# mLSTM decay matrix, state scaling and gating queued behind later VectorE work; five weight parts ahead and later row rounding at the FFN's edges

## The chip, the cores and the metric

The kernel runs on one core of a Trainium2 chip. The metric is the device time of one execution in microseconds (us). Engine names are those of the profile: PE is TensorE's matmul, PEld its weight load, DVE is VectorE, ACT is ScalarE, POOL is GpSimd, SP is SyncE, which here only issues DMAs. Each engine works through its own queue of instructions, whose order is fixed when the kernel is built.

## What is computed

One inference step of a two-layer decoder, for 1024 new prompt tokens and 8 decode tokens, in float32. Layer 0 mixes tokens with an mLSTM, layer 1 with multi-head latent attention (MLA); each is followed by a SwiGLU FFN. Cut to what the change touches:

```
def mlstm_chunk(C, n, m, q, k, v, i_pre, log_f):          # one chunk, one head
    b = cumsum(log_f)
    log_intra = where(causal, b[:, None] - b[None, :] + i_pre[None, :], -inf)
    m_t = maximum(b + m, max(log_intra, -1))
    s = (q @ k.T) * exp(log_intra - m_t[:, None])          # decay matrix times scores
    num = exp(b + m - m_t) * (q @ C) + s @ v
    den = exp(b + m - m_t) * (q @ n) + sum(s, -1)
    h = num / maximum(abs(den), exp(-m_t))
    C = w_C * C + k.T @ (w_s * v)                          # state update
...
h = rmsnorm_per_head(h) * g_head
y = (sigmoid(o) * h) @ w_out                               # gating, output projection
...
def swiglu(x): g, u = split(x @ w_gate_up); return (silu(g) * u) @ w_down
```

The decode tokens scale and update a stored state per request in the same way.

## The kernel before, in words

**Precision.** Each float32 operand of a matmul is split into a rounded high part (ScalarE, line 117) and a rest (VectorE, line 118; with a gain factor lines 120 and 121); a product is three matmuls, high by high, low by high, high by low (`mm3`, lines 134 to 136). So every weight tile costs a load on SyncE's queue, a ScalarE and a VectorE operation before PE can use it. PE accumulates in PSUM, from which VectorE or ScalarE must copy a result before its bank is used again.

**Order of the work.** The program is written in one thread of Python. The framework builds each engine's queue from it: the instructions of one engine are put in an order by the program's order and by when an estimate says that their inputs are ready, so an instruction whose inputs are thought to be there early can be queued ahead of earlier work. On the chip this order is then fixed. `tc.issue_after(ins)` adds an ordering edge: what the block issues on the engine of `ins` is queued behind `ins`. It does not wait for `ins` to finish, and it binds no other engine.

**mLSTM.** After the projections of q, k and v (`proj_v(0..7)`, eviction at line 447), 16 chunk steps run: 8 chunks of 128 tokens by 2 groups of 4 heads (loop in `mlstm`, step `mlstm_chunk`). A step
- takes `Gb`, gate values broadcast to all partitions by a DMA on ScalarE's queue (`decay`, line 608; four buffers), and makes the decay matrix in place: four VectorE operations (line 625), then an exponential on ScalarE (line 626);
- multiplies the scores, fresh in PSUM, into it (line 633), turns k and v (kt, line 639; vn, line 645), and makes numerator and denominator on PE (lines 660, 662);
- updates the state C (PE line 672, VectorE lines 676 or 678, four operations);
- normalises: denominator (687 to 692), an inverse square root of eleven short operations (198 to 203), line 694, and the scaled output `hn` (line 697);
- in the next step, turns `hn` back on PE (701) and copies it over v (702).

Between the steps PE works on other products: in steps 1 to 8 the output gate's projection `proj_o` (three PSUM results in two banks, evicted at line 464, tanh at 465, stored by DMA), in steps 9 to 14 tiles of the output projection for the first 512 tokens (`op_tile`, line 863). The decode tokens' state is worked on in between by a generator, `mlstm_sample`: load the state of a request, scale it (line 799), add the new outer product (800), store it (801), and take its product with q (781). The gating of half 1 of the tokens (`gated`, lines 480, 120, 121) runs in steps 12 to 14, three, three and two heads, each loaded (`loaded`, line 475) just before.

**FFN.** The gate and up products use a Strassen-like scheme: per block of 128 columns (`f`, 22 of them) seven products (`PRODUCTS`) of seven weight parts (`operands`, which makes sums of weight quarters at lines 1032, 1033, 1038, 1039 and splits them) with seven sums of the activations, the "forms" (`forms`, lines 943 and 946, split at 117 and 118). The seven products share two PSUM banks per half of the tokens, so the first product's result must be copied out (line 1078) before the third starts the same bank again, and the second's (line 1080) before the fourth. The first two blocks are done without forms (`gate_up_half`); in `out_proj` the parts of block 2 are made among the forms of half 1, and `gate_up` takes them from `self.early`. The last four blocks (`fs`, 18 to 21) go a simpler way: `keep` splits their activations (ScalarE and VectorE) for a plain last product.

Of the kernel before, what the change touches and what calls it, by code (L numbers as in the profile page):

```python
# [13 lines left out]
ALU = mybir.AluOpType  # L14
# [4 lines left out]
P = 128  # L19
# [9 lines left out]
NF = DFF // P  # L29
# [62 lines left out]
class Kern:  # L92
# [309 lines left out]
    def mlstm(self, xz, rs, early):  # L402
# [41 lines left out]
        turned = self.gates(p1, pg, gi, lf, bcol)  # L444
        def proj_v(j):
            def ev(c, cs, ps):
                nc.vector.tensor_tensor(v[:, j, cs], ps, rs[:, cs], op=ALU.mult)
            proj(1024 + j * P, ev)

        for j in range(8):  # L450
            proj_v(j)
            if j == 4:
                turned()
        pg.release()
        o_d = self.t(self.dp, [P, 8, T], "o_d")
        pi = self.pool("mi")
# [17 lines left out]
        def loaded(og, i, h, zs):  # L474
            nc.sync.dma_start(og, o_d[:, h, 512 * i + zs.start:512 * i + zs.stop])
            return og, i, h, zs

        def gated(og, i, h, zs):
            cs = slice(512 * i + zs.start, 512 * i + zs.stop)
            nc.vector.scalar_tensor_tensor(og, og, 1.0, v[:, h, cs], op0=ALU.add, op1=ALU.mult)  # L480
            self.split(z[i][0][:, h, zs], z[i][1][:, h, zs], og, self.gcol(self.G_HEAD + h))


        smp = self.mlstm_sample(ms, q, k, v)
        last = None
        first, rest = OPC[1]
        due = [self.decay(pi, 0, 0)]
        for i in range(16):
            if i < 15:
                due.append(self.decay(pi, (i + 1) // 2, (i + 1) % 2))  # L490
            g = self.mlstm_chunk(pi, i // 2, i % 2, q, k, v, *due.pop(0))
            next(g)
            if i == 8:
                next(smp, None)
            if 1 <= i <= 8:
                proj_o(i - 1)
            elif 9 <= i <= 14:
                self.op_tile(0, i - 9, ("mm",))
            if last:
                next(last, None)  # L500
            last = g
            for _ in range(0 if i > 8 else 2 if i == 3 else 1):
                next(smp, None)
            if i == 8:
                ms.release()
                self.rp.release()
                self.zp.release()
                z = self.half_z(512)
                og = self.t(self.xq, [P, KT, 512], "x")
                for h in range(8):  # L510
                    gated(*loaded(og[:, h], 0, h, slice(0, 512)))
                self.op_open(self.mlstm_w_out[0], z)
                self.X[0] = self.t(self.xq, [P, KT, 512], "x")
                self.SS[0] = self.t(self.xq, [P, 512], "ss")
                self.sq[0] = self.xq
                self.op_residual(0, nc.sync)

            if 12 <= i <= 14:
                for h in range(3 * i - 36, min(8, 3 * i - 33)):
                    gated(*loaded(ob()[:, :256], 1, h, first))  # L520

        tiles = [self.t(pi, [P, 4, L], "Gb", bufs=4).rearrange("p h t -> p (h t)")] + [ob() for _ in range(3)]
        tiles += [self.t(pi, [P, 4, 129], "vn", bufs=3).rearrange("p h t -> p (h t)") for _ in range(2)] + [ob() for _ in range(2)]
# [91 lines left out]
    def mlstm_chunk(self, pi, c, hg, q, k, v, Gb, wb):  # L615
# [5 lines left out]
        a_t, ws_t, em_t = (self.tok[:, c, r, h4] for r in range(3))  # L621

        E = Gb
        for h in range(4):
            V.scalar_tensor_tensor(E[:, h], Gb[:, h], a_t[:, h:h + 1], self.ct[:, C_MM:C_MM + P], op0=ALU.subtract, op1=ALU.max)
        nc.scalar.activation(E, E, AF.Exp, scale=-1.0)
        for hh in range(2):
            ps = self.mmt("sc")[:, :2 * L]
# [44 lines left out]
        for h in range(4):  # L673
            r = slice((h % 2) * 64, (h % 2) * 64 + 64)
            if c == 0:
                V.tensor_copy(C[r, h], ps[r, h // 2])
            else:
                V.scalar_tensor_tensor(C[r, h], C[r, h], wc[r, h // 2:h // 2 + 1], ps[r, h // 2], op0=ALU.mult, op1=ALU.add)
        if c == NCK - 1:
            for hh in range(2):  # L680
                r = slice(hh * 64, hh * 64 + 64)
# [22 lines left out]
    def mlstm_sample(self, pi, q, k, v):  # L704
# [91 lines left out]
        for b in range(NS):  # L796
            yield
            Ct, vb = nxt
            V.tensor_tensor(Ct, Ct, wsb[:, 0, b].unsqueeze(2).to_broadcast([P, 4, P]), op=ALU.mult)
            V.tensor_tensor(Ct, Ct, vb, op=ALU.add)  # L800
            nc.sync.dma_start(self.C_s[0, b].rearrange("(q r) d e -> (r d) q e", r=2), Ct)
            if prev:
                products(*prev)
            if b < NS - 1:
                nxt = fetch(b + 1)
            prev = (b, Ct)
# [66 lines left out]
    def out_proj(self, layer):  # L873
        nc = self.nc
        V = nc.vector
        self.fz = self.pool("fz")
        xp = self.pool("xp")
        for i in range(1, -layer, -1):
            self.X[i] = self.t(xp, [P, KT, 2 * PW[i]], f"x{i}")
        nt = self.pool("nt")  # L880
        for i in range(1 - layer, 2):
            self.SS[i] = self.t(nt, [P, 2 * PW[1]], f"ss{i}")
            self.sq[i] = nt
        self.F = {}
# [24 lines left out]
        self.fc = self.pool("fc", side="right")  # L909
        self.nf = self.pool("nf", side="right")  # L910
        gen = self.forms(1, self.X[1], self.SS[1], g0)
        self.u = {}
        self.nr = self.no = 0
        wg = self.ffn_w_gate_up[layer]
        self.gate_up_half(wg, 0, gen)
        self.gate_up_half(wg, 1)
        ops = self.operands(wg, 2)
        parts = []
        for step in range(5):
            next(gen, None)  # L920
            parts += [next(ops) for _ in range((0, 2, 1, 1, 0)[step])]
        self.early = ops, parts
        self.nf.release()
        nt.release()
        xp.release()
# [119 lines left out]
    def gate_up(self, wg, f, parts, down=iter(()), skip=0, steps=(1, 1)):  # L1045
# [9 lines left out]
            ops = self.operands(wg, f)  # L1055
            ahead = [next(ops) for _ in range(2 if f < 3 else 1)]
        for s, bank, first in PRODUCTS:
            ahead.append(next(ops, None))
            w = ahead.pop(0)
            for i in parts:  # L1060
                pw = PW[i]
# [13 lines left out]
                    X[i] = self.t(gu, [P, PW[1]], "gt", bufs=2)[:, :pw]  # L1075
                u, x = U[i], X[i]
                if s == 0:
                    nc.scalar.copy(u[:, 0], ps)
                elif s == 4:
                    V.tensor_tensor(u[:, 0], u[:, 0], ps, op=ALU.add)  # L1080
                    nc.scalar.activation(u[:, 0], u[:, 0], AF.Silu)
# [113 lines left out]
    def ffn(self, layer):  # L1195
# [27 lines left out]
            o = lambda x: x[:, 512 * i:512 * i + 2 * PW[i]].rearrange("p (c t) -> p c t", c=2)  # L1223
            self.split(o(self.act[f][0]), o(self.act[f][1]), self.u[f, i])

        for i in range(2):
            keep(fs[0], i)
        self.gate_up(wg, fs[2], (0, 1), (keep(fs[1], i) for i in range(2)))
        self.gate_up(wg, fs[3], (0, 1))
        for f in fs[2:]:  # L1230
            for i in range(2):
# [831 lines left out]
```

## Time and profile before

| | us |
|---|---|
| median of 3 runs | 2632.49 |
| lowest and highest | 2632.12, 2639.99 |
| profiled execution: its own time | 2652.47 |
| its span, first to last instruction | 2650.7 |
| PE busy | 2520.7 |
| VectorE busy | 1861.4 |
| ScalarE busy | 1326.0 |

How to read the profile. A row of the timeline gives start, duration, engine, line, operation, out<-in by the program's names, shape, count, and in square brackets how long the engine was idle before it and what ended that. A row of waits gives who waited for whom, the total, the number of times and the longest. A row of stretches gives length, and the busy time of each engine with its number of instructions, then the granted clock of TensorE as a share of full speed, and the DMA engines' share and rate. The chain of waits follows the work that ended last back to what released it. PE's ends are modelled, and some matmul records can be missing.

### The profile page before, as it was taken

How to read it: one execution, taken by the hardware profiler on the slowest of the kernel's cores; microseconds unless marked ns; L12 is line 12 of the kernel's file. 1: busy time of each engine (PE TensorE's matmuls, PEld its weight loads, DVE VectorE, ACT ScalarE, POOL GpSimd, SP SyncE). 2: the span in 40 equal slices, each digit the busy share in tenths (PEclk: the TensorE clock that was granted, in tenths of full speed). 3: DMA queues.
4: the chain of work that ended last, by engine and by line, in shares of the span. 5: the costliest groups of instructions: out<-in, count | busy, mean ns of one | idle time of the engine just before them, and what ended most of it. 6: DMA issues, size and time to landing. Idle time of an engine off the chain costs nothing.

```text
span 2650.7 us, 54288 instructions
## 1 busy us (share of the span) xinstructions
PE 2520.7 (95%) x21151; PEld 2377.0 (90%) x21151; DVE 1861.4 (70%) x4491; ACT 1326.0 (50%) x3281; POOL 570.8 (22%) x588
## 2 busy tenths in 40 slices
PE   8998989999999999999988888988999999999998
PEld 8998977999999999999976667767899999999998
DVE  4345668897777777566657766767597877777755
ACT  4122234456565666454344454645355665656543
POOL 1001102202111111122335444541210111111102
PEclk9999999999999999999989999999999999999999
DMA  5123444527666566554657666664634656665653
GB/s 192 40 68 89 135 136 128 164 65 139 133 124 129 113 118 134 113 161 149 203 209 255 208 225 234 223 240 134 199 94 107 133 117 128 128 133 113 124 127 115
DMA packets 343128, 382.88 MB, mean 144 GB/s; under 512 B 23465, under 2 KB 275502, under 8 KB 334550
## 3 DMA queue, kind: packets, MB, share of 16 engines
q0 software_dynamic: 58688, 180.35, 29.2%
q1 hardware_dynamic: 258982, 182.30, 22.8%
q10 hardware_dynamic: 25200, 16.75, 2.4%
q8 instruction: 166, 2.72, 0.4%
q14 instruction: 92, 0.75, 0.1%
HBM read 253.63 MB, written 125.70 MB: 143 GB/s over the span
## 4 chain that ended last, share of the span: by engine, by line
PE 73%; DVE 11%; DMA 7%; ACT 5%; issue 3%; POOL 1%; SPq 0%; another core or an unknown queue 0%; ACTq 0%; POOLq 0%; DVEq 0%
PE sc L134 13%; PE sc L136 13%; PE sc L135 13%; PE mm L134 6%; PE mm L136 5%; PE mm L135 5%; PE ss L1873 2%; PE ss L134 2%; PE ss L136 2%; PE ss L135 2%; DVE tt L1841 2%; DMA Gb<-G_d 2%; PE ss L1848 2%; DVE wl L118 1%; PE mm L1744 1%
## 5 line engine op out<-in xcount | busy, mean ns | idle before, releaser
L1178 POOL DMA_DIRECT2D x_d<-wl x72 | 86.8, 1205 | 1001.8 <-DVE wl L1177 347.1
L117 ACT ACTIVATE wh<-wr 128x512 fp32r<-128x512 f32 (+2 forms) x167 | 133.4, 800 | 179.9 <-PE mm L135 111.0
L1841 DVE STREAM_TRANSPOSE tt<-nat 128x1024 f32<-128x1024 f32 x128 | 153.9, 1223 | 16.7 <-PE ss L1848 13.0
L118 DVE TENSOR_TENSOR wl<-wr,wh 128x1024 fp32r<-128x1024 f32 (+2 forms) x80 | 93.0, 1164 | 27.1 <-ACT wh L117 26.4
L134 PE MATMUL mm<-zh,wh 128*128 128x344 f32 x320 | 104.4, 326 | 6.5 <-DVE ot L464 6.5
L118 DVE TENSOR_TENSOR b<-u,b 128x256 fp32r<-128x256 f32 (+1 forms) x252 | 103.2, 423 | 9.2 <-ACT b L117 7.8
L117 ACT ACTIVATE b<-u 128x256 fp32r<-128x256 f32 (+1 forms) x252 | 99.0, 415 | 15.8 <-PE ss L136 6.3
L1178 POOL DMA_DIRECT2D x_d<-st x72 | 104.6, 1453 | 5.0 <-DVE dC L118 3.8
L1848 PE MATMUL ss<-tt,qbd 128*32 128x128 f32 x2560 | 94.0, 280 | 11.8 <-issue 6.3
L118 DVE TENSOR_TENSOR wh<-S,wh 128x512 fp32r<-128x512 f32 x108 | 74.6, 691 | 42.9 <-ACT wh L117 42.8
L135 PE MATMUL mm<-zl,wh 128*128 128x344 f32 x320 | 103.5, 324 | 0.0
L136 PE MATMUL mm<-zh,wl 128*128 128x344 f32 x320 | 103.3, 323 | 0.0
L1848 PEld LDWEIGHTS ss<-tt,qbd 128*32 128x32 f32 x2560 | 72.2, 112 | 29.5 <-issue 12.9
L117 ACT ACTIVATE wh<-S 128x512 fp32r<-128x512 f32 x108 | 68.0, 630 | 59.6 <-PE sc L136 39.7
L1744 PE MATMUL mm<-wh,vt 128*128 128x256 f32 (+1 forms) x320 | 79.4, 309 | 10.0 <-ACT wh L117 5.6
L134 PE MATMUL sc<-zh,wh 128*128 128x344 f32 x256 | 83.5, 327 | 2.9 <-ACT wh L117 2.7
L136 PE MATMUL sc<-zh,wl 128*128 128x344 f32 x256 | 82.7, 323 | 0.7 <-DVE wl L118 0.7
L135 PE MATMUL sc<-zl,wh 128*128 128x344 f32 x256 | 82.7, 323 | 0.0
L1873 PE MATMUL ss<-nat,pz 128*32 128x256 f32 x1024 | 68.6, 401 | 11.2 <-ACT pz L1869 10.6
L1703 ACT ACTIVATE wr<-sc,mx,rqt 128x512 f32<-128x512 f32 (+2 forms) x96 | 64.2, 674 | 26.8 <-DVE mx L1698 13.1
L1744 PEld LDWEIGHTS mm<-wh,vt 128*128 128x128 f32 x320 | 58.0, 205 | 21.7 <-ACT wh L117 9.7
L1833 POOL DMA_INDIRECT nat<-in_cache_latent_dram,idx x64 | 60.8, 950 | 75.2 <-PE ss L1873 61.5
(1078 smaller groups left out, 10666.1 us busy)
## 6 DMA issues: line engine op xcount, KB each, us to landing
wr<-in_ffn_w_gate_up_dram SPq DMA_DIRECT2D x96, 512.0 KB
x_d<-st POOLq DMA_DIRECT2D x72, 520.0 KB
x_d<-wl POOLq DMA_DIRECT2D x72, 512.0 KB
dr<-in_ffn_w_down_dram SPq DMA_DIRECT2D x72, 256.0 KB
wr<-in_mlstm_w_in_dram SPq DMA_DIRECT2D x24, 512.0 KB
wr<-in_mlstm_w_out_dram SPq DMA_DIRECT2D x16, 512.0 KB
q<-qn_d SPq DMA_DIRECT2D x28, 256.0 KB
wr<-in_mla_w_o_dram SPq DMA_DIRECT2D x14, 512.0 KB
```

What stands on the lines that cost most here:

```text
L117: ins = nc.scalar.activation(hi, src, AF.Copy)
L118: self.low = e.tensor_tensor(lo, src, hi.bitcast(F32), op=ALU.subtract)
L134: mm(ps, wh, xh, start=start, stop=False, **kw)
L135: mm(ps, wh, xl, start=False, stop=False, **kw)
L136: self.last = mm(ps, wl, xh, start=False, stop=stop, **kw)
L1178: nc.gpsimd.dma_start(self.x_d[:, 2 * dp:2 * dp + 2, 512 * i:512 * i + 2 * PW[i]], st[i], accum_op=ALU.add)
L1703: nc.scalar.activation(px[:, ks], o, AF.Exp, bias=mx[:, 0:1], scale=f, accum_out=sm[:, c:c + 1])
L1744: nc.tensor.matmul(o, x, y, start=i == 0, stop=i == len(ops) - 1)
L1833: nc.gpsimd.indirect_dma_start(out=nat[:, s].rearrange("p s c -> p (s c)"), out_offset=None, in_=lat, in_offset=ix)
L1841: V.transpose(out=tt, in_=src.rearrange("p s (c i) -> p c s i", i=32))
L1848: nc.tensor.matmul(psS[32 * j:32 * j + 32, u * P:u * P + P], self.qbd[:, b, cb], tt[:, c, 4 * j:4 * j + 4].rearrange("p s k -> p (s k)"), ...
L1873: nc.tensor.matmul(psV[32 * j:32 * j + 32], pz[:, j, i], keys[i // 4][:, j * 4 + i % 4], start=i == 0, stop=i == 7)
```

## The change

Six edits; no arithmetic is added or removed.

1. `self.pin` is set to the last eviction of V column 6, and the four VectorE operations of a decay matrix (line 625) are issued under `issue_after(self.pin)`. After each step `self.pin` is that step's last state update. So the first decay matrix is queued behind V column 6, and each other one behind the state update of the step before.
2. The scaling of a decode request's state (line 799) is queued behind `hn` of the current step.
3. The gating of half 1: its loads are issued one step earlier (steps 11 to 13), and the gating in steps 12 to 14 is queued behind `hn` of that step.
4. In `out_proj`, five instead of four weight parts of block 2 are made ahead, the fifth before the last forms (activation sums 5 and 6).
5. In `gate_up` of block 20, ScalarE's part of the weights that is prepared at the third product is queued behind the copy of the first product (line 1078).
6. In `ffn`, the rows of blocks 18 and 19 are no longer split ahead of block 20 and at its first product, but one by one in its second product.

```diff
@@ mlstm
             def ev(c, cs, ps):
-                nc.vector.tensor_tensor(v[:, j, cs], ps, rs[:, cs], op=ALU.mult)
+                self.pin = nc.vector.tensor_tensor(v[:, j, cs], ps, rs[:, cs], op=ALU.mult).ins
...
+            if j == 6:
+                pin = self.pin
+        self.pin = pin
...
-            if 12 <= i <= 14:
-                for h in range(3 * i - 36, min(8, 3 * i - 33)):
-                    gated(*loaded(ob()[:, :256], 1, h, first))
+            with self.tc.issue_after(self.hn.ins):
+                for x in held:
+                    gated(*x)
+            held = [loaded(ob()[:, :256], 1, h, first) for h in range(3 * i - 33, min(8, 3 * i - 30)) if i > 10]
@@ mlstm_chunk
-        for h in range(4):
-            V.scalar_tensor_tensor(E[:, h], Gb[:, h], a_t[:, h:h + 1], self.ct[:, C_MM:C_MM + P], op0=ALU.subtract, op1=ALU.max)
+        with self.tc.issue_after(self.pin):
+            for h in range(4):
+                V.scalar_tensor_tensor(E[:, h], Gb[:, h], a_t[:, h:h + 1], self.ct[:, C_MM:C_MM + P], op0=ALU.subtract, op1=ALU.max)
...
+        self.pin = ins.ins
@@ mlstm_sample
-            V.tensor_tensor(Ct, Ct, wsb[:, 0, b].unsqueeze(2).to_broadcast([P, 4, P]), op=ALU.mult)
+            with self.tc.issue_after(self.hn.ins):
+                V.tensor_tensor(Ct, Ct, wsb[:, 0, b].unsqueeze(2).to_broadcast([P, 4, P]), op=ALU.mult)
@@ out_proj
-            parts += [next(ops) for _ in range((0, 2, 1, 1, 0)[step])]
+            parts += [next(ops) for _ in range((0, 2, 1, 2, 0)[step])]
@@ gate_up
-            ahead.append(next(ops, None))
+            with self.tc.issue_after(copied) if f == NF - 2 and s == 3 else nullcontext():
+                ahead.append(next(ops, None))
...
-                    nc.scalar.copy(u[:, 0], ps)
+                    copied = nc.scalar.copy(u[:, 0], ps).ins
@@ ffn
-        for i in range(2):
-            keep(fs[0], i)
-        self.gate_up(wg, fs[2], (0, 1), (keep(fs[1], i) for i in range(2)))
+        self.gate_up(wg, fs[2], (0, 1), (keep(f, i) for f in fs[:2] for i in range(2)), 4)
```

More of the change, by code (lines that the diff above doesn't have):

```diff
@@ L485, in mlstm @@
         last = None
+        held = []
         first, rest = OPC[1]
@@ L675, in mlstm_chunk @@
             if c == 0:
-                V.tensor_copy(C[r, h], ps[r, h // 2])
+                ins = V.tensor_copy(C[r, h], ps[r, h // 2])
             else:
-                V.scalar_tensor_tensor(C[r, h], C[r, h], wc[r, h // 2:h // 2 + 1], ps[r, h // 2], op0=ALU.mult, op1=ALU.add)
+                ins = V.scalar_tensor_tensor(C[r, h], C[r, h], wc[r, h // 2:h // 2 + 1], ps[r, h // 2], op0=ALU.mult, op1=ALU.add)
+        self.pin = ins.ins
         if c == NCK - 1:
```

## The prediction

> **What bounds the kernel now.** I read the page first (busy shares), then the busy time by stretches, then the waits of TensorE and VectorE, then the chain of waits, and last the timeline where a wait was long. One core runs, and its page says:
>
> ```profile
> span 2650.7 us, 54288 instructions
> PE 2520.7 (95%) x21151; PEld 2377.0 (90%) x21151; DVE 1861.4 (70%) x4491; ACT 1326.0 (50%) x3281; POOL 570.8 (22%) x588
> ```
>
> TensorE (PE) is busy for all but 130 us. The change removes no arithmetic, so it can only win idle time of PE, and what that idle time does to PE's clock. The edits touch three places: the last V projection and the 16 mLSTM chunk steps (here 203 to 452 us), the start of each FFN (554 and 1987), and the last two column blocks of each FFN (1116 and 2550). Stretches of the first place, cut at the transposes that end a step (columns: length, then busy us of PE, PEld, DVE, ACT, POOL, then granted clock, DMA share, GB/s):
>
> ```profile
> 203.40:211.74 8.34, 5.06 (x21) 4.77 (x22) 4.83 (x9) 2.64 (x3) 0.37 (x2) 0.80 0.50 115
> 239.32:261.45 22.13, 18.08 (x117) 16.70 (x114) 13.43 (x49) 5.71 (x17) 4.10 (x6) 0.92 0.45 107
> 261.45:279.92 18.47, 16.84 (x124) 16.10 (x122) 11.74 (x37) 5.60 (x17) 2.01 (x4) 1.00 0.43 122
> 279.92:299.73 19.81, 19.81 (x133) 19.09 (x130) 12.13 (x40) 5.48 (x17) 1.16 (x4) 0.91 0.53 151
> 299.73:318.69 18.96, 16.95 (x125) 16.06 (x122) 11.90 (x37) 5.82 (x18) 3.81 (x6) 1.00 0.46 122
> 318.69:336.20 17.51, 16.86 (x125) 16.10 (x123) 10.94 (x37) 5.59 (x17) 0.96 (x3) 1.00 0.40 114
> ```
>
> A step with an output-gate projection needs 16.85 us of PE at full clock, and takes 17.5 to 22. No engine is full, so something waits. The waits of PE from 200 to 372 us, and below them those of DVE from 180 to 372 (total, times, longest):
>
> ```profile
> PE mm L134 <- DVE ot L464: 6.5, 5, 2.0
> PE sc L134 <- ACT wh L117: 2.7, 1, 2.7
> PE sc L660 <- ACT vn L645: 2.7, 1, 2.7
> ```
>
> ```profile
> DVE Gb L625 <- DMA Gb<-G_d: 32.2, 9, 6.2
> DVE s_C L799 <- DMA s_C<-in_state_mlstm_C_dram: 8.1, 5, 4.3
> ```
>
> PE waits for VectorE to empty PSUM (L464). VectorE itself stood still nine times in front of a decay matrix (L625) whose gate values had not landed, 32.2 us together. Does that stop matter? The chain of waits over 200 to 372 us begins with it:
>
> ```profile
> by line: DMA Gb<-G_d 21.1%; PE mm L134 11.3%; PE mm L135 10.6%; PE mm L136 10.3%; issue 3.4%; DVE Gb L625 3.3%; PE ss L781 3.0%; DMA s_vb<-vs_d 3.0%; DVE C L678 2.7%; PE sc L631 2.3%; PE sc L660 2.2%; DVE ot L464 2.0%; PE sc L136 1.9%; PE s
> ```
>
> A fifth of that stretch is a load that nobody needs yet. One step of VectorE's timeline, and the exponential on ScalarE that follows a decay matrix:
>
> ```profile
> 309.38 1.14 DVE L625 SCALAR_TENSOR_TENSOR Gb<-Gb,tok,ct 128x128 f32<-128x128 f32 x4 [3.74 <-DMA Gb<-G_d]
> ...
> 310.72 1.41 DVE L678 SCALAR_TENSOR_TENSOR C<-C,wc,ss 64x129 f32<-64x129 f32 x4
> ...
> 314.23 0.52 DVE L464 TENSOR_TENSOR ot<-mm,rs 128x344 f32<-128x344 f32 x1
> ```
>
> ```profile
> 310.55 0.63 ACT L626 ACTIVATE Gb<-Gb 128x512 f32<-128x512 f32 x1 [4.06 <-DVE Gb L625]
> ```
>
> The decay matrix at 309 belongs to a later step, stands ahead of this step's state update (L678), its normalisation and the eviction L464, and holds them all for 3.74 us.
>
> **The change, part by part.** The same instructions get other places in the engines' queues. An ordering edge waits for nothing: it only says behind which instruction of its own engine another one is queued.
>
> The price of a clock drop comes first, since it recurs. Stretches of equal length; PE's instructions are in the first bracket, the granted clock is the last number but two:
>
> ```profile
> 1116.27:1119.69 3.42, 3.42 (x19) 3.42 (x18) 1.05 (x3) 1.13 (x3) 0.00 (x0) 0.50 0.56 160
> 1119.69:1123.10 3.41, 3.41 (x30) 3.41 (x30) 0.69 (x1) 0.91 (x2) 0.00 (x0) 1.00 0.00 0
> 1986.67:1990.09 3.42, 3.17 (x15) 3.17 (x16) 3.42 (x10) 2.17 (x7) 0.00 (x0) 0.50 0.77 218
> 2549.87:2553.28 3.41, 2.91 (x13) 2.92 (x14) 1.91 (x5) 1.48 (x5) 0.00 (x0) 0.50 0.84 214
> ...
> 245.87:249.29 3.42, 3.25 (x15) 3.28 (x16) 0.38 (x1) 0.87 (x6) 0.00 (x0) 0.50 0.52 116
> ...
> 208.33:211.74 3.41, 3.41 (x14) 3.41 (x14) 1.29 (x2) 0.00 (x0) 0.00 (x0) 0.50 0.79 206
> ```
>
> 19 matmuls instead of 30: 11 x 3.41/30 = 1.25 us lost for each half-clock stretch behind a wait.
>
> (1) First decay matrix behind V column 6. Before, four decay matrices go ahead and hold VectorE and ScalarE; the weight split for column 6 is late, and PE idles 8.34 - 5.06 = 3.28 us at half clock afterwards. Gone: 3.28 + 1.25 = 4.53. Three of the four matrices move into the steps; they cost 1.14 us of VectorE each where it is busy 13.4 of 22.1 us or less, so nothing. Bounds 0 and 4.53.
>
> (2) Decay matrix behind the previous step's state update, and state scaling behind the normalisation, in the steps with a projection. The idle time of PE there is 4.05, 1.63, 2.01 and 0.65 in the rows above (length less PE). I take the three large ones, 7.69, and one clock drop (245.87): 8.94. The step at 279.92 has a clock drop with PE never idle; I leave it. Bounds 0 and 6.5 + 2.7 + 1.25 = 10.45. The later state scaling also delays the state's store on SyncE's queue, with the loads of the next broadcast behind it, and GpSimd's product of that broadcast; all three are needed only a step (17 us) later. If that cover went, every us by which they came late would be one of PE.
>
> (3) Gating of half 1, loaded a step earlier and queued behind the normalisation. Here the steps are short:
>
> ```profile
> 403.09:414.19 11.10, 10.35 (x66) 8.27 (x67) 9.33 (x35) 4.69 (x16) 2.48 (x4) 1.00 0.46 118
> 414.19:426.28 12.09, 10.45 (x68) 8.25 (x66) 9.76 (x35) 5.35 (x18) 2.48 (x4) 1.00 0.33 98
> 426.28:439.70 13.42, 11.81 (x67) 9.58 (x66) 12.28 (x47) 6.46 (x20) 2.25 (x2) 0.87 0.52 146
> 439.70:451.61 11.91, 10.43 (x68) 8.25 (x67) 11.05 (x41) 5.14 (x17) 4.74 (x6) 1.00 0.41 115
> ```
>
> ```profile
> DVE Gb L625 <- DMA Gb<-G_d: 3.2, 2, 1.8
> ```
>
> PE's idle time is 5.48, but VectorE is busy 42.42 of 48.52 us and close to the bound itself. Only its two waits for decay rows, 3.2 us, can go; I take half, 1.6. Its eight loads go out a step earlier on SyncE's queue, ahead of weights that PE needs a step later; I count nothing. What queues behind the moved gating: the next step's state update, and ScalarE's rounding of the gated rows; so the bounds are -2 (the sign reversed) and 5.48 + 1.25 = 6.73.
>
> (4) FFN start, a fifth weight part ahead of the last forms; and (5) FFN end, the activations' rows out of the way. PE's waits in both layers:
>
> ```profile
> 553.88 0.39 PE L134 MATMUL sc<-f2h,wh 128*128 128x256 f32 x1 [2.49 <-ACT wh L117]
> ...
> 1115.90 0.39 PE L134 MATMUL sc<-f3h,wh 128*128 128x256 f32 x1 [3.19 <-ACT v L1078]
> ...
> 1986.92 0.58 PE L134 MATMUL sc<-f2h,wh 128*128 128x256 f32 x1 [2.45 <-ACT wh L117]
> ...
> 2550.37 0.58 PE L134 MATMUL sc<-f3h,wh 128*128 128x256 f32 x1 [3.21 <-ACT v L1078]
> ```
>
> ```profile
> 552.46 0.69 DVE L1039 TENSOR_TENSOR S<-wr,wr 128x512 f32<-128x512 f32 x1
> ...
> 553.67 0.42 DVE L1080 TENSOR_TENSOR u<-u,sc 128x256 f32<-128x256 f32 x1
> ```
>
> ```profile
> 1113.41 2.19 ACT L117 ACTIVATE a<-u 128x512 fp32r<-128x512 f32 x4
> 1115.50 0.63 ACT L1078 COPY v<-sc 128x256 f32<-128x256 f32 x2
> ```
>
> (4): product 5 waits for the part made at 552.46, behind a form on VectorE. Earlier, it lets product 5 run at once, until 554.1, when L1080 has emptied the bank for product 4. I take 2.0 of each wait and the second layer's clock drop, 5.25; bounds 0 (if product 4 comes first, its bank still waits for L1080) and 2.49 + 2.45 + 1.25 = 6.19. The last forms slip by the part's own VectorE work, by my estimate three operations like L1039, 2.1 us; they feed products 6 and 7, which stand at least one product behind (24 matmuls of 3.41/30, 2.7 us).
>
> (5): four rounded rows (2.19 us) and a weight part stand before the copy that empties product 1's bank. After the change the rows come behind it: 3.19 + 3.21 + 2 x 1.25 = 8.90. Their VectorE halves now stand near L1080, for which product 4 waits; for that I take off 0.5 in each layer: 7.9, bounds 0 and 8.9.
>
> Sum: 4.53 + 8.94 + 1.6 + 5.25 + 7.9 = 28.2 us. The profiled execution has 2650.7 us between its first and last instruction and took 2652.47, of which 28.2 leaves 2624.3. The runs without profile have a median of 2632.49; the same waits taken from it give 2604.3.
>
> Whether the clock terms belong in it is where a rule stands against a row. In the rows above a wait of 3.19 us ends at 1115.90, and the clock is 0.50 from 1116.27 on; the sum by the rows is 28.2. The Trainium skill, page "TensorE: Matmul & The Clock Gate", section "HAM oscillation — how this bites in real kernels", gives as its abstract rule that PE's idle gaps should stay under about 3.4 us; by it these shorter waits would not have dropped the clock, the sum would be 21.9, and this trace does not agree.
>
> **The rivals.** *The waits change owner in the steps.* PE's waits of part 2 name an eviction that also stands behind eleven short normalisation operations; if those and not the loads decide, parts 2 and 3 give nothing, and 17.7 remains: 2614.8. For it: the eviction at 314.23 comes after some of them. Against it: 21.1% of the chain is the load.
>
> *Shorter waits leave the clock alone.* Then the five drops have other causes and stay: 28.2 - 5 x 1.25 = 21.9, 2610.5. Against it: each of the five stands beside a wait of 2.45 to 3.28 us. The rule of the Trainium skill's page "TensorE: Matmul & The Clock Gate" that stands under the sum would give this case.
>
> *The change does not do what it says.* An ordering edge binds one engine's queue only; if ScalarE and PE keep their order, only the tail's rows move: 7.9, 2624.6.
>
> *Slower: the decay matrix comes just in time.* It was made early, now it cannot start before the previous state update. If the pair L625 and L626 (1.14 + 0.63 = 1.77) ends after the scores are ready, 15 steps pay 26.6; with parts 1, 4 and 5 still won (17.7) that is 2641.4. It decides where less than 1.77 us lies between state update and score product. The update above ends at 312.1, that step's end is 318.69: 6.6 us at least. I hold it unlikely.
>
> **How the numbers follow.** Forecast 0.66, owner change 0.16, clock 0.04, only the tail 0.09, just in time 0.05. About 0.3% (7.9 us) is what a measurement can tell from no change. The first three are faster; of the fourth a quarter. So faster 0.88, same 0.07, slower 0.05. Range: all upper bounds give 4.53 + 10.45 + 6.73 + 6.19 + 8.90 = 36.8, 2595.7; the runs before differ by 7.9 (2632.12 to 2639.99), so 2588 below. Above, the owner change, 2614.8, and the same spread, with the tail-only case: 2626.
>
> **What would show it.** Right: no wait of L625 for its rows over 1 us after 215; steps of 16.9 to 17.6; L625 just after L678; no idle PE over 1 us near 206, 554, 1116 and their twins, with clock 1.00. Wrong: score products (L633) waiting for L626, or evictions L464 that still hold PE; a wait at product 4 for L1080; or a new half-clock stretch.

## The result and the profile after

Before and after ran side by side: 2634.93 us median before (2632.12 to 2639.99, 4 runs), 2609.72 after (2606.56 to 2614.76, 4 runs). The ratio is 0.9904, 95% interval 0.988 to 0.9928: 25.2 us less, between 19.0 and 31.6. The forecast was 2604.3, 28.2 us less. The later runs stood on three chips, where the kernel before had medians of 2635.57, 2660.50 and 2654.78, so kernels are compared by ratios to it, and stages by landmarks in the trace. Line numbers are those of each kernel: in the changed one the eviction L464 is L467, the decay matrix L625 is L631, the squares are L672 and the state scaling L799 is L807.

The profiled execution after took 2606.56 us. Its page:

```profile
span 2604.6 us, 54290 instructions
PE 2496.4 (96%) x21151; PEld 2361.3 (91%) x21151; DVE 1858.4 (71%) x4491; ACT 1327.5 (51%) x3281; POOL 573.7 (22%) x588
```

The span is 46.1 us shorter, more than the runs say: the execution profiled before, 2652.47 us, took longer than any of its four runs, and the one after is the fastest of its four. So first where these two executions differ. The table gives the start of PE's work at some landmarks in us, and the difference to before:

| landmark | before | after | |
|---|---|---|---|
| scores of the first chunk step | 220.00 | 216.82 | -3.2 |
| end of step 1 (start of its transposes) | 261.45 | 261.01 | -0.4 |
| end of step 5 | 336.20 | 329.02 | -7.2 |
| output projection of half 1 | 468.46 | 460.52 | -7.9 |
| FFN of layer 0, first product of block 2's rows | 553.88 | 549.26 | -4.6 |
| its last product, after all blocks | 1151.80 | 1142.72 | -9.1 |
| output projection of layer 1 | 1852.14 | 1813.91 | -38.2 |
| end of the span | 2650.70 | 2604.56 | -46.1 |

The stretch from 1152 to 1852, from the last product of layer 0's FFN through the MLA layer to its output projection, holds 29 of the 46 us, and no edit touches it; it is called the MLA layer below. A second profile of the kernel before, below, is 17.7 us shorter there. The rest is 9.1 us ahead of it and 7.9 behind it.

The stretches of the V projection and of steps 1 to 5 after (columns as before):

```profile
203.40:211.74 8.34, 6.90 (x43) 6.42 (x42) 5.20 (x10) 2.48 (x3) 1.27 (x2) 1.00 0.54 147
235.85:261.01 25.16, 17.72 (x115) 16.56 (x114) 12.59 (x43) 5.71 (x17) 1.89 (x4) 0.86 0.30 73
261.01:277.59 16.58, 16.58 (x124) 16.11 (x122) 10.48 (x37) 5.60 (x17) 1.90 (x4) 1.00 0.48 136
277.59:295.85 18.26, 18.26 (x132) 17.64 (x130) 12.89 (x40) 5.60 (x17) 3.04 (x5) 1.00 0.59 170
295.85:312.43 16.58, 16.58 (x124) 16.11 (x122) 10.49 (x37) 5.60 (x17) 1.97 (x4) 1.00 0.49 134
312.43:329.02 16.59, 16.59 (x124) 16.12 (x122) 10.49 (x37) 5.59 (x17) 1.90 (x4) 1.00 0.50 133
```

Four of the five steps now have no idle PE at all. The first, 25.16 us, is 3 us longer than before: a new stall. The two largest waits of PE and of VectorE over the windows that the prediction used (200 to 372, 180 to 372):

```profile
PE mm L134 <- DVE ot L467: 6.0, 1, 6.0
PE ss L650 <- ACT v L709: 1.6, 2, 1.4
```

```profile
DVE dn L694 <- ACT dn L669: 16.8, 7, 2.7
DVE ssq L697 <- ACT junk L672: 12.4, 4, 8.8
```

The 32.2 us in front of a decay matrix are gone from VectorE's list. In their place VectorE waits for ScalarE's sums in the normalisation, nearly all of it idle time that costs PE nothing, except for one wait of 8.8 us. That one is the stall; read engine by engine it is a chain. First a decay matrix's load on ScalarE's queue (ACTq is its issue of DMAs) and, right behind it on SyncE's (SPq), the load that GpSimd waits for; then GpSimd, ScalarE, VectorE and PE:

```profile
239.09 0.45 ACTq L613 DMA_DIRECT2D Gb<-G_d  x1
239.68 1.25 SPq L797 DMA_DIRECT2D s_vb<-vs_d  x2
```

```profile
251.12 1.04 POOL L798 TENSOR_TENSOR s_vb<-s_vb,s_kw 128x512 f32<-128x512 f32 x1 [15.40 <-DMA s_vb<-vs_d]
252.11 0.72 POOL L656 TENSOR_TENSOR qw<-q,wb 128x256 f32<-128x256 f32 x1
252.82 0.18 POOL L658 COPY wc<-wb 128x2 f32<-128x2 f32 x1
```

```profile
252.87 0.58 ACTq L617 DMA_DIRECT2D wb<-wi_d  x1
253.49 0.28 ACT L672 ACTIVATE junk<-sc 128x128 f32<-128x128 f32 x1 [9.98 <-POOL wc L658]
```

```profile
253.90 0.16 DVE L697 TENSOR_TENSOR ssq<-ssq,r 128x4 f32<-128x4 f32 x1 [8.77 <-ACT junk L672]
...
255.10 0.52 DVE L467 TENSOR_TENSOR ot<-mm,rs 128x344 f32<-128x344 f32 x1
```

```profile
255.67 0.65 PE L134 MATMUL mm<-zh,wh 128*128 128x344 f32 x1 [6.03 <-DVE ot L467]
```

GpSimd's product for the stored state (L798) waits for its broadcast, issued at 239.68, until 251.12. Behind it in GpSimd's queue stand qw and wc, the last readers of a `wb` buffer. The load of the next `wb` (L617) needs that buffer, and it is issued from ScalarE's queue: until it can go, ScalarE's squares (L672) stand behind it. VectorE waits for them, with the eviction L467 behind, and PE for that. The Trainium skill, page "TensorE: Matmul & The Clock Gate", section "Architectural detail: the array is 16× 32×32, not 1× 128×128", says that ScalarE and VectorE are strict first-in, first-out; this trace agrees, with 9.98 us of ScalarE idle behind one DMA issue.

The FFN edges after (first the rows in which product 5 starts, then stretches of the length of the clock's steps behind them):

```profile
549.26 0.38 PE L134 MATMUL sc<-f2h,wh 128*128 128x256 f32 x1 [0.80 <-ACT gt L1092]
...
1946.55 0.38 PE L134 MATMUL sc<-f2h,wh 128*128 128x256 f32 x1 [0.58 <-ACT gt L1092]
```

```profile
549.26:552.67 3.41, 3.41 (x27) 3.38 (x28) 3.41 (x7) 1.98 (x7) 0.00 (x0) 1.00 0.76 230
1946.55:1949.96 3.41, 3.41 (x27) 3.37 (x28) 3.41 (x7) 1.97 (x7) 0.00 (x0) 1.00 0.76 226
```

2.49 and 2.45 us became 0.80 and 0.58, at full clock. Of the waits of 3.19 and 3.21 us at each FFN's end none is left. This is all of the waits of PE from 545 to 1150:

```profile
PE sc L134 <- ACT gt L1092: 0.8, 1, 0.8
PE sc L136 <- DVE wh L118: 0.3, 1, 0.3
```

### The profile page after: what moved, and what is told of

The parts are those of the page before. It is cut to its first block, busy times and chain, and to the rows that moved or that the text cites. A ratio compares the mean times of both kernels' runs of the same rounds, so it can differ in the third digit from the quotient of the medians.

```text
span 2604.6 us, 54290 instructions
## 1 busy us (share of the span) xinstructions
PE 2496.4 (96%) x21151; PEld 2361.3 (91%) x21151; DVE 1858.4 (71%) x4491; ACT 1327.5 (51%) x3281; POOL 573.7 (22%) x588
## 5 line engine op out<-in xcount | busy, mean ns | idle before, releaser
L1848 DVE STREAM_TRANSPOSE tt<-nat 128x1024 f32<-128x1024 f32 x128 | 153.6, 1222 | 23.4 <-DMA nat<-in_cache_latent_dram,idx 13.8
L1855 PE MATMUL ss<-tt,qbd 128*32 128x128 f32 x2560 | 86.6, 276 | 4.2 <-DVE tt L1848 2.3
L1855 PEld LDWEIGHTS ss<-tt,qbd 128*32 128x32 f32 x2560 | 69.7, 110 | 16.8 <-DVE tt L1848 10.8
(1078 smaller groups left out, 10650.7 us busy)
```

What stands on the lines that cost most here:

```text
L1848: V.transpose(out=tt, in_=src.rearrange("p s (c i) -> p c s i", i=32))
L1855: nc.tensor.matmul(psS[32 * j:32 * j + 32, u * P:u * P + P], self.qbd[:, b, cb], tt[:, c, 4 * j:4 * j + 4].rearrange("p s k -> p (s k)"), ...
```

## The experiments

**The kernel before again**, one profile, to learn how far two executions of one kernel agree.

> The kernel before once more, unchanged, for a second profile. The two profiles at hand differ by 46.1 us in span but the medians by 25.2; between the first MLA scores and the first product of layer 1's output projection they take 510.6 us (before) and 482.7 us (after), although the change touches nothing there. If that is the execution and not the change, this profile has another length there (485 to 505 us), and agrees with the first profile within 0.5 us up to the first row product that ends FFN 0 (1151.8 us). If the change made MLA faster, it shows 510 us again.

It took 2637.81 us. Ahead of the MLA layer its landmarks agree with the first profile within 3.2 us, not the 0.5 that I had expected (220.14, 261.19, 336 us for step 5, 471.58, 557.04, 1154.78). The MLA stretches of the two (length, busy time of the engines, clock):

```profile
1151.80:1852.14 700.34, 628.19 (x6443) 526.98 (x6441) 480.83 (x1078) 352.37 (x877) 283.34 (x297) 0.95 0.62 210
```

```profile
1154.78:1837.38 682.60, 620.11 (x6442) 525.68 (x6441) 479.63 (x1080) 352.69 (x877) 282.80 (x297) 0.95 0.63 215
```

The same work took 700.3 and 682.6 us; the chip of the first profile is not on record. So differences of a few us in the whole time can't be laid to an edit from single profiles; the landmarks ahead of the MLA layer tell edits apart from about 3 us on.

**The state scaling back in its place** (edit 2 undone):

```diff
-            with self.tc.issue_after(self.hn.ins):
-                V.tensor_tensor(Ct, Ct, wsb[:, 0, b].unsqueeze(2).to_broadcast([P, 4, P]), op=ALU.mult)
+            V.tensor_tensor(Ct, Ct, wsb[:, 0, b].unsqueeze(2).to_broadcast([P, 4, P]), op=ALU.mult)
```

> The changed kernel without edit 2 (the state scaling is not queued behind the normalisation). Theory: the new wait of 6.03 us at 255.67 us comes from edit 2: the later scaling makes the state's store and the next broadcast load later, GpSimd waits for that load ahead of its product for the step, so the step's buffer of inter-chunk weights comes free late, ScalarE's DMA issue stands in its queue, and the squares, the normalisation and the eviction stand behind it. Then the wait of 6 us is gone, the waits of line 799 for the state come back (up to 8 us of VectorE, of PE at most 3), and FFN 0's end comes 3 to 8 us earlier than 1142.7; the time is 2602 to 2607. Rival: ScalarE's DMA issue is held up by the moved decay matrices (edit 1); then the wait of about 6 us stays and the time is 2610 or more.

2611.95 us (2609.13 to 2616.94, 6 runs), ratio 0.9913 (0.9893 to 0.9933). The wait of 6.03 us is gone, so the later scaling is a condition of the stall. But the step has another wait in its place, and is still long:

```profile
PE ss L650 <- ACT v L709: 3.3, 1, 3.3
```

```profile
235.76:257.49 21.73, 18.44 (x117) 17.56 (x115) 13.85 (x52) 6.71 (x19) 4.03 (x6) 0.84 0.49 125
```

Step 1 ends at 257.49 instead of 261.01, step 4 at 312.01 instead of 312.43: three steps later the gain is gone. At the FFN of layer 0 it is 2.0 us (547.25), and at its end 2.0 (1140.68), where 3 to 8 were expected; two profiles of one kernel differed by more. What this edit is worth, these runs can't tell.

**The gating back in its place** (edit 3 undone):

```diff
-            with self.tc.issue_after(self.hn.ins):
-                for x in held:
-                    gated(*x)
-            held = [loaded(ob()[:, :256], 1, h, first) for h in range(3 * i - 33, min(8, 3 * i - 30)) if i > 10]
+            if 12 <= i <= 14:
+                for h in range(3 * i - 36, min(8, 3 * i - 33)):
+                    gated(*loaded(ob()[:, :256], 1, h, first))
```

> The changed kernel without edit 3 (gating of half 1 loaded and queued as before). The prediction's part 3: the edit won 1.6 us, so without it 2611.3. Rival: in the steps 9 to 15 and the switch to half 1 VectorE is the bound, the gating only moved into the next step's update, and the waits there (9.3 us in the changed kernel against 5.9 before) are its price; then without it half 1's output projection starts 2 to 5 us earlier than 460.5, and the time is 2605 to 2608.

2608.70 us (2600.73 to 2619.52, 6 runs), ratio 0.9903 (0.9876 to 0.9929). The FFN of layer 0 starts at 542.95 instead of 549.26 and ends at 1136.57 instead of 1142.72: without the edit 6.2 us are won there, which the whole time, with its spread of 19 us, does not show. The place is the start of half 1's output projection. Stretches from there to the next transposes, before, after, then without the gating edit:

```profile
468.11:482.53 14.42, 14.13 (x119) 13.95 (x118) 11.43 (x31) 7.86 (x15) 1.33 (x3) 1.00 0.86 274
```

```profile
460.17:480.88 20.71, 17.74 (x132) 17.14 (x131) 14.49 (x35) 8.73 (x17) 2.68 (x3) 0.92 0.71 215
```

```profile
458.78:473.20 14.42, 14.13 (x119) 13.95 (x118) 11.34 (x31) 7.87 (x15) 1.34 (x3) 1.00 0.89 274
```

And what VectorE, SyncE, ScalarE and PE do there after. The first two rows are the last two gated heads (256 columns) and the load behind them, the third is the load of such a row without the gating edit:

```profile
451.35 0.75 DVE L483 SCALAR_TENSOR_TENSOR ot<-ot,v 128x256 f32<-128x256 f32 x2
452.85 0.79 SPq L478 DMA_DIRECT2D ot<-o_d  x2
```

```profile
435.91 0.32 SPq L478 DMA_DIRECT2D ot<-o_d  x1
```

```profile
463.05 0.52 ACT L120 ACTIVATE zh1h<-ot,g 128x264 fp32r<-128x264 f32 x1 [2.43 <-DVE ot L483]
463.47 1.04 ACT L117 ACTIVATE wh<-wr 128x1024 fp32r<-128x1024 f32 x1
```

```profile
462.58 0.43 DVE L483 SCALAR_TENSOR_TENSOR ot<-ot,v 128x264 f32<-128x264 f32 x1 [2.58 <-DMA ot<-o_d]
```

```profile
464.56 0.39 PE L134 MATMUL sc<-zh1h,wh 128*128 128x256 f32 x1 [0.97 <-ACT wh L117]
466.36 0.38 PE L136 MATMUL sc<-zh1h,wl 128*128 128x256 f32 x1 [1.29 <-DVE wl L118]
```

The rows of the remaining columns (264 wide) use the buffers of the gated heads, so two of their loads go out at 452.85, behind the gating that the edit moved; without it two loads into these buffers go out at 431.93 and 435.91. The gating of the remaining columns waits for a row that arrives late; ScalarE's rounding of that row and, behind it in the queue, the weight split for which PE waits, are late with it. Without the edit the first row of these columns is gated at 453.73 instead of 459.24. The other profiles agree, apart from those with a later decay matrix (below), where PE takes this work in another order. From the first product of half 1's output projection to the first FFN product of block 2 (460.52 to 549.26 in the changed kernel), the kernels with the gating as before take 85.4 to 85.5 us, or 83.8 to 83.9 with the FFN edits. With the gating edit they take 88.6, or 86 to 90 with the FFN edits.

**The gating edit alone**, on the kernel before:

> The kernel before with the gating edit alone: half 1's rows loaded a step earlier and gated behind the next step's normalisation. The prediction's part 3 gives 1.6 us less, with bounds of 6.73 less and 2 more. The finding from taking the edit out of the changed kernel says the opposite: the half-1 output projection starts with its rounded rows late, and the layer-0 FFN starts 4 to 6 us later than in the kernel before (553.88 to 557.04 us): 2637 to 2641 us. If the cost belongs to the edit only together with the shorter steps of the changed kernel, the start of the FFN stays where it was, within 2 us.

2665.36 us (2660.85 to 2674.56, 12 runs) against 2660.50 (17 runs): ratio 1.0024, 1.001 to 1.0039, so 6.3 us slower, 2.6 to 10.3. The FFN starts at 561.64 instead of 553.88 (557.04 in the second profile). The edit costs by itself, in the kernel with the long steps too.

**The decay edits alone**, on the kernel before (edit 1, with the pin of each step; scaling, gating and FFN as before):

```diff
+        with self.tc.issue_after(self.pin):
+          for h in range(4):
...
+        self.pin = ins.ins
```

> The kernel before with the decay edits alone (first matrix behind V column 6, the others behind the previous step's state update; state scaling, gating and FFN as before). By the prediction's parts 1 and 2 this is 4.53 us and nearly all of 8.94: the layer-0 FFN starts 9 to 13 us earlier than 553.88, 2620 to 2624 us against 2633. By the sum of the runs so far (whole change 25.2 us less, FFN edits alone 18.7 less, gating 6 more, scaling near 0) it is 10 to 13 us less. By the rival that waits change owner only part 1 remains: 3 to 4.5 us less.

2643.43 us (2641.76 to 2649.1, 7 runs) against 2654.78 (12 runs): ratio 0.9959, 0.9942 to 0.9977, which is 10.8 us of 2632, 6 to 15. The FFN of layer 0 starts at 541.66, 12.2 us earlier (15.4 against the second profile). Steps 1 to 4:

```profile
233.82:254.28 20.46, 17.32 (x117) 16.43 (x115) 14.08 (x53) 6.66 (x19) 3.00 (x5) 0.92 0.51 133
254.28:270.86 16.58, 16.58 (x124) 16.11 (x123) 11.00 (x37) 5.59 (x17) 2.03 (x4) 1.00 0.51 136
270.86:290.26 19.40, 18.52 (x131) 17.62 (x130) 11.92 (x40) 5.59 (x17) 1.68 (x4) 1.00 0.55 147
290.26:306.84 16.58, 16.58 (x124) 16.11 (x122) 11.04 (x37) 5.59 (x17) 3.37 (x6) 1.00 0.60 148
```

They sum to 73.02 us; before they took 79.37. The decay matrix was what held VectorE.

**The FFN edits alone** (4, 5 and 6, on the kernel before):

> The kernel before with edits 4, 5 and 6 alone (the FFN's edges). The prediction's parts 4 and 5: 13.2 us together, 2621.8; by the profiles of before and after 1.7 + 2.45 + 1.9 + 1.25 us at the start and 2 x 4.45 at the end, 13 to 14 in all. Rival, the start of the FFN gives nothing because product 4's bank comes free no earlier: 8.9 us, 2626. If the mLSTM edits gave nothing at all: 2610.

2616.89 us (2614.24 to 2625.82, 6 runs) against 2635.57: ratio 0.993, 0.9909 to 0.9951, 18.7 us less. By landmarks it is less: 2.2 us at the start of layer 0's FFN, 4.6 more at its end, and 7.0 in the stretch behind the MLA layer, 13.8 together. The other 4.9 show at no landmark outside the MLA layer; by the interval of the ratio the edits win 12.9 to 24.0 us, so 13.8 is within it.

**The decay matrix still later** (the changed kernel, each matrix behind the previous step's `hn` instead of its state update), against the rival that it comes just in time:

```diff
-        self.pin = ins.ins
...
+        self.pin = self.hn.ins
```

> The changed kernel with each decay matrix queued behind the previous step's normalisation (hn) instead of its state update, a few us later on VectorE. The rival of the prediction: the matrix comes just in time, and a step pays once less than 1.77 us lies between its end and the scores. If the slack is the 6.6 us that the prediction read, the normalisation's 3 to 4 us leave 2 us or more and nothing is paid: the changed kernel's time within 3 us. If the slack is used up already, the scores wait for the exponential (L632) in the steps: 15 steps at up to 1.77 us, 10 to 27 us more, and the page shows waits of PE or VectorE on Gb from ScalarE.

2628.30 us (2626.26 to 2631.01, 4 runs) against 2660.50: ratio 0.9877, 0.9852 to 0.9902. The exponential costs nothing: VectorE, which multiplies the scores in, has no wait for it between 215 and 460 us. The step that had the stall takes 16.18 us:

```profile
235.52:251.70 16.18, 16.11 (x116) 15.02 (x114) 13.13 (x46) 5.82 (x17) 2.01 (x4) 1.00 0.44 113
```

In GpSimd's queue qw now stands ahead of the product for the stored state, and ScalarE's DMA issue goes without a stop:

```profile
245.56 0.73 POOL L656 TENSOR_TENSOR qw<-q,wb 128x256 f32<-128x256 f32 x1
248.10 1.04 POOL L798 TENSOR_TENSOR s_vb<-s_vb,s_kw 128x512 f32<-128x512 f32 x1 [1.81 <-DVE ssq L698]
```

```profile
246.33 0.58 ACTq L617 DMA_DIRECT2D wb<-wi_d  x1
246.96 0.28 ACT L672 ACTIVATE junk<-sc 128x128 f32<-128x128 f32 x1 [1.07 <-POOL qw L656]
```

The FFN of layer 0 starts at 543.32, 5.9 us ahead of the changed kernel.

**The product behind wc** (GpSimd's L798 with an ordering edge behind the last wc copy):

```diff
-            nc.gpsimd.tensor_tensor(vb, vb, kw[:, b].unsqueeze(2).to_broadcast([P, 4, P]), op=ALU.mult)
...
+            with self.tc.issue_after(self.wci) if self.wci else nullcontext():
+                nc.gpsimd.tensor_tensor(vb, vb, kw[:, b].unsqueeze(2).to_broadcast([P, 4, P]), op=ALU.mult)
```

> The changed kernel, with GpSimd's product for the recurrent state's update (s_vb times kw) queued behind the next step's copy wc instead of ahead of qw and wc. The work is the same. Theory of the chain: the later state scaling makes the s_vb load late, GpSimd waits for it, and qw, wc, a DMA issue on ScalarE's queue, the squares and the eviction L467 stand behind it. Then the wait of 6.03 us at 255.67 and the half-clock stretch after it go, step 2 starts its transposes at 257 to 258 instead of 261.0, and GpSimd's qw no longer follows a wait for s_vb. What of it lasts is at most the 6.03 and 1.25, more likely 0 to 3 us by the start of the layer-0 FFN, since the kernel with the early scaling won 3.5 us at the same place and had lost 3.1 of it two steps later: 2605 to 2609 us. Rival: the wait at 255.67 is the eviction's own place on VectorE, behind the normalisation: then it stays above 4 us, and the time is the changed kernel's within 2 us.

2638.81 us (2632.08 to 2647.84, 6 runs), ratio 0.9918 (0.9895 to 0.9942). The wait of PE is still there with 6.2 us, but the queue was not changed where it mattered: the wc behind which the product was put is that of an earlier step, and at 251.74 the product again stood ahead of qw (252.74) and wc (253.45). The run decides nothing.

**The broadcast's load ahead of the store** on SyncE's queue:

```diff
+            if b < NS - 1:
+                nv = fetch_v(b + 1)
             nc.sync.dma_start(self.C_s[0, b].rearrange("(q r) d e -> (r d) q e", r=2), Ct)
...
-                nxt = fetch(b + 1)
+                nxt = fetch_C(b + 1), nv
```

> The changed kernel with the two loads of the next s_vb broadcast issued on SyncE's queue ahead of the store of the scaled state instead of behind it. The same work. (In the kernel that queued GpSimd's product behind wc, the product at 251.74 us still stood ahead of qw and wc, so that run changed nothing at the place in question.) Theory of the chain: the store waits for the late scaling, and the load behind it makes s_vb late; now the load is issued near 230 us, GpSimd's product runs by 240, wc and the DMA issue of wb follow, and the wait of 6.03 us at 255.67 with its half-clock stretch is gone; step 2 begins at 251 to 255 instead of 261.0, as far as the kernel with the later decay matrix got (251.70). What lasts by the start of the layer-0 FFN is 0 to 6 us: a ratio to the kernel before of 0.988 to 0.990 (the changed kernel: 0.9904). Rival: the product waits because GpSimd's queue is held by something else, or the wait lies in the order of L697 and L467 on VectorE alone: then the wait stays within 1 us of 6.03 and step 2 begins at 260 to 262.

2631.16 us (2627.22 to 2637.24, 4 runs) against 2654.78: ratio 0.9919 (0.9895 to 0.9943). The wait is 4.67 us, and step 1 ends at 258.38: between the two expectations. SyncE's queue shows that the load still went out behind the store:

```profile
237.57 0.40 SPq L814 DMA_DIRECT2D out_C_s_dram<-s_C  x1
238.49 1.25 SPq L800 DMA_DIRECT2D s_vb<-vs_d  x2
```

The broadcast has two buffers, and the load fills the one that the state's update (VectorE's L811, 236.97 to 237.65) had just read. So what makes the load late is that update; the store that still stood ahead of it can account for at most the 0.84 us between the update's end and the load, and "store ahead of load" as a link of the chain falls. The layer-0 FFN starts at 543.97 and ends at 1137.45 here, about 5.3 us ahead of the changed kernel, though the wait is only 1.4 us shorter; where that comes from stays open.

**Three attempts at a faster kernel**: without the gating edit and with the product edge; without it and with the later decay matrix; the last also with the load ahead of the store.

> The changed kernel without the gating edit, and with GpSimd's s_vb product queued behind the next step's copy wc. The same work. If both costs are what the stages showed (6.15 us for the gating up to the end of the layer-0 FFN, 0 to 3 us for the product), that landmark comes at 1133.5 to 1136.6 us instead of 1142.7, and the time is 6 to 9 us below the changed kernel's: 2600 to 2604. Rival: what is won before the half-1 output projection is given back in the long MLA stretch, as the kernel without the gating edit suggests by its times (2608.70): then the landmark is early and the time stays at 2607 to 2610.

> The changed kernel without the gating edit, and with each decay matrix behind the previous step's normalisation. If the two gains are separate (6 us by the layer-0 FFN's end for each), that landmark comes at 1130 to 1133 us (changed kernel 1142.72, later decay alone 1136.72, without gating alone 1136.57), and the ratio to the kernel before is 0.984 to 0.987. If they are the same gain (both only take the loss at 460 to 549 us away), the landmark stays at 1136 to 1138 and the ratio at 0.987 to 0.990.

> The kernel without the gating edit and with the later decay matrices, with the s_vb loads also ahead of the state's store. If the later decay matrix already freed GpSimd and the ScalarE queue in the second step, nothing changes: step 2 begins within 1.5 us of 251.7 and the time within 3 us of that kernel's. If the loads still hold up other steps, up to 4 us more are won before the layer-0 FFN.

Ratios 0.9909 (0.9884 to 0.9934), 0.9922 (0.9902 to 0.9943), 0.9921 (0.9903 to 0.9938). The layer-0 FFN ends at 1139.43, 1137.40 and 1139.08, where the later decay matrix alone has 1136.72 and the removed gating alone 1136.57. In the first the wait of PE is still there with 6.4 us, as in the run with the product edge alone. The two gains do not add up: the layer-0 FFN starts at 543.32 with the one, 542.95 with the other and 543.85 with both, each about 6 us ahead of the changed kernel. The second kernel shows where a lead is lost: PE begins half 1's output projection at 451.69, 7.4 us ahead of the kernel that only lacks the gating edit, and then has a wait that the other does not have:

```profile
465.66 0.43 DVE L483 SCALAR_TENSOR_TENSOR ot<-ot,v 128x264 f32<-128x264 f32 x1 [3.06 <-DMA ot<-o_d]
```

```profile
466.69 0.59 PE L134 MATMUL mm<-zh1h,wh 128*128 128x264 f32 x1 [2.74 <-ACT zh1h L120]
```

It reaches the remaining columns before their last rows have landed, waits 2.74 us, and runs at a clock of 0.56 to 0.59 from 466 to 474. The kernel with the later decay matrix alone has the same wait there (2.35 us at 468.12). None of these kernels is told apart from the changed one by its time.

## Why the prediction was right, and where it was not

**The direction and the bulk were right**: 28.2 us forecast, 25.2 measured (19.0 to 31.6), inside the range. That the sum came so close is partly luck: one term has the wrong sign, another was put at nothing, and some us have no term. Two of the prediction's own signs of being wrong appeared: an eviction that holds PE (6.03 us at 255.67), and a new half-clock stretch (467).

**Part 1**, 4.53 us: 3.2 at the first scores, 2.9 to 5.2 in the other kernels with this edit. The stretch at 203.40 has 1.44 us of idle PE left, not none, at clock 1.00 instead of 0.80.

**Part 2**, 8.94 us: the decay half was right. Parts 1 and 2 forecast 13.47 together, and the decay edits alone brought the FFN's start forward by 12.2 and took 10.8 off the time. The mechanism is the one read from the chain: a matrix that waited for a load that nobody needed yet. The scaling edit was costed at nothing, because its consumers "are needed only a step later", with the price named if that cover went. It did go in one step: 6.03 us at 255.67. The update freed the broadcast's buffer at 238.74, its load was issued at 239.68, and the product that needs it ran at 251.12. Two kinds of kernel removed that wait: one took the scaling back, the others, with the later matrix, had qw ahead of the product. As far as these show, the stall needs both, a late load and a product ahead of qw. Why the load took up to 11.4 us, when it was there in at most 6.4 with the later matrix, is not shown, but the traces have a pattern. In the five kernels with the stall (PE's wait is 3.2 to 6.4 us in them) the load went out 0.6 us behind a decay matrix's load, and the product ran 10.1 to 11.8 us later. In the other kernels with the decay edits that load came 4 us earlier, or later, and the product ran 5.6 to 7.1 us after the issue. No run moves that load alone. Taking the scaling edit out of the changed kernel won 2.0 us at the FFN, so most of the stall's price did not last.

**Part 3**, 1.6 us: wrong in sign, and outside its bound of -2. The edit costs 6.3 us alone (2.6 to 10.3) and 6.2 us at the FFN's end in the changed kernel. The step that failed is "what queues behind the moved gating", bounded at -2 by the sign reversed. I looked at the four short steps and not at what follows them: the gated rows of the remaining columns take over the buffers, so a gating that ends later delays their loads, their rounding on ScalarE, and the first weight split of half 1. A bound from the waits inside a stretch does not hold for what the stretch hands on.

**Parts 4 and 5**, 5.25 and 7.9 us: right. The starts' waits shrank by 1.69 and 1.87 (2.0 taken), the ends' waits of 3.19 and 3.21 went whole, product 4 does not wait for L1080 (L1089 after), and the half-clock stretches at 1116, 1987 and 2550 are gone. Alone these edits gave 13.8 us by landmarks against 13.15 forecast.

**The sum by stages** is 4.6 + 4.5 + 7.9 = 17.0 us outside the MLA layer, where the terms promised 28.2. The difference is the gating (1.6 forecast, 6.2 lost: 7.8), the scaling (2.0, no more than two profiles of one kernel differ) and parts 1 and 2 by about 1. Against the second profile of the kernel before the same sum is 20.0, inside the measured interval. So the measured time is better than the landmarks by 5 to 8 us, and the FFN edits alone were better than theirs by 5; neither is clear of the noise, and neither shows at a landmark outside the MLA layer. That layer's length goes more with the chip than with the edits, in single profiles: 682.6 us without the FFN edits and 674.6 to 678.5 with them on one chip, 700.0 and 699.2 to 707.5 on the second, 705.8 and 693.6 to 703.1 on the third. Whether the FFN edits do something there, or its own spread does, stays open.

**The clock terms.** Where PE's waits went, the half-clock stretches behind them went too, as the rows had it, and the rival that keeps them is out. By the rule of the Trainium skill, page "TensorE: Matmul & The Clock Gate", section "HAM oscillation — how this bites in real kernels", waits under about 3.4 us would not have mattered; the trace does not agree: half-clock stretches stood behind waits of 2.45 to 3.21 us and went with them.

**The rivals.** Waits that change owner: in four of five steps no wait of PE is left. Only the tail: the steps moved. Just in time: the matrix could go later still without a wait for its exponential, so the slack read from the row (6.6 us) was there.

## What to carry to other kernels

An instruction that waits for a load is only as cheap as what is queued behind it; look for such heads of queues in the chain before costing the load itself. For an instruction that is moved later, follow every buffer it frees: the price of edit 3 and of the scaling edit came by way of a buffer, a load and a third engine, in one case after the stretch that I had bounded. Compare stages by landmarks: terms of opposite sign, and a layer whose length differs by 18 us between two profiles of one kernel, can make a sum look right.

## What the runs showed of the hardware

Three things I had not expected. A DMA issue on ScalarE's queue whose buffer was not free held that engine's arithmetic for 9.98 us. PE's two waits of 0.97 and 1.29 us, within 2.8 us, were followed by one half-clock stretch (clock 0.50 from 467.13 to 470.54), so in this place no single wait of 2.45 us stood before it. And the MLA layer, with the same instructions, took 682.6 and 700.3 us in two profiles at the same mean clock, 0.95.
